# Weighted sum of two expert outputs: a store of its own for tile 0's first two tokens, and the last tile's weight load moved to another queue

## The chip, the cores and the metric

The kernel runs on one core of a Trainium2 chip. A core has several engines, each with its own instruction queue: VectorE (DVE in the profile), ScalarE (ACT), GpSimd (POOL), TensorE (PE, unused here) and SyncE (SP, which only waits and issues transfers). Transfers between the chip's main memory (HBM) and the on-chip memory with its 128 partitions are carried by 16 DMA engines, which all queues share. The metric is the device time of one execution in microseconds.

## The reference

There are 16 x 1024 = 16384 tokens. For each one the input holds two rows of 512 float32 numbers, from two experts, and two weights. The output is the weighted sum of the two rows:

```python
def reference(expert_outputs, combine_weights):   # (16,1024,2,512), (16,1024,2)
    weights = combine_weights[..., np.newaxis]
    return np.sum(expert_outputs * weights, axis=2).astype(np.float32)
```

The input is 67.1 MB, the output 33.6 MB, and a token needs 1024 multiplications and 512 additions.

## The kernel before, in words

Each partition handles 128 tokens. The first 120 of them (`main`) lie together in HBM for each partition, and are worked in ten tiles of 12 (`J`); the last eight (`LAST`) come from the end of the tensor and form tile 10, the last one. A tile `et` is 128 partitions x 12 tokens x 1024 numbers, 48 KB per partition. The pool `in` has four buffers, so tiles 0 to 3 are loaded without waiting, and the load of tile g (line 69) waits until the store of tile g-4 has landed.

All loads are issued by SP, in order (line 69). Tile 0's load is split in two: two tokens (called load 0a in what follows, rows of 4 KB) and the other ten (load 0b). All weights lie in one small tile `wt`; two transfers on ACT's queue fill it at the start (line 55): the weights of the first 120 tokens, and the 8 KB of the last tile. A warm-up ACTIVATE (line 60) follows.

Tiles 0 to 8: DVE multiplies the whole tile by the weights in place (line 78), then adds the two halves of each token (line 79). The result `ot` lies in the same buffer, packed at its front. ACT's queue issues the store (line 80), so that a store waits on DVE, and behind it wait all later stores.

Tile 9: ACT multiplies the first expert's rows, one token at a time (line 86), DVE the second's (line 101), and DVE adds (line 102). Tile 10: ACT multiplies the first expert's row of each token (line 86) and DVE multiplies and adds in one instruction (line 90). SP issues these two stores (line 103), behind all the loads. A framework orders the instructions within each queue and sets the semaphores.

Of the kernel before, what the change touches and what calls it, by code (L numbers as in the profile page):

```python
# [1 line left out]

# [4 lines left out]


@with_exitstack
def kernel(  # L10
    ctx: ExitStack,
    tc: tile.TileContext,
    expert_outputs: bass.AP,
    combine_weights: bass.AP,
    out: bass.AP,
):

    nc = tc.nc  # L20
    b, s, k, h = expert_outputs.shape
    assert k == 2
    n = b * s
    P = nc.NUM_PARTITIONS
    per = n // P
    assert per * P == n
    J, LAST = 12, 8
    main = per - LAST
    assert main % J == 0
    eo = expert_outputs.rearrange("b s k h -> (b s) (k h)")  # L30
    cw = combine_weights.rearrange("b s k -> (b s) k")
    o = out.rearrange("b s h -> (b s) h")

    def rows(x):

        a = x[0 : P * main, :].rearrange("(p t) f -> p t f", p=P)
        b = x[P * main : n, :].rearrange("(p t) f -> p t f", p=P)
        return lambda t, c: a[:, t : t + c, :] if t < main else b[:, t - main : t - main + c, :]

    eo, cw, o = rows(eo), rows(cw), rows(o)  # L40

    dt = mybir.dt.float32
    mult = mybir.AluOpType.mult
    add = mybir.AluOpType.add
    copy = mybir.ActivationFunctionType.Copy

    last = main // J

    wpool = ctx.enter_context(tc.tile_pool(name="w", bufs=1))
    ipool = ctx.enter_context(tc.tile_pool(name="in", bufs=4))  # L50

    wt = wpool.tile([P, per * k], dt)

    for t, c in ((0, main), (main, LAST)):
        nc.scalar.dma_start(
            out=wt[:, k * t : k * (t + c)].rearrange("p (t k) -> p t k", k=k), in_=cw(t, c)
        )

    warm = wpool.tile([P, 1], dt)
    nc.scalar.activation(out=warm, in_=nc.const_aps.tensor(1.0, (P, 1), dt), func=copy)  # L60

    for g in range(last + 1):
        et = ipool.tile([P, J, k * h], dt)

        ot = et.rearrange("p j f -> p (j f)")[:, 0 : J * h].rearrange("p (j f) -> p j f", f=h)
        t0, c = g * J, J if g < last else LAST

        for a, m in ((0, 2), (2, c - 2)) if g == 0 else ((0, c),):
            nc.sync.dma_start(  # L69
                out=et[:, a : a + m],  # L70
                in_=eo(t0 + a, m),
                max_dma_last_dim=k * h * 4 if g + a == 0 else None,
            )
        if g < last - 1:

            wb = wt[:, g * J * k : (g + 1) * J * k].unsqueeze(2).to_broadcast([P, J * k, h])
            ek = et.rearrange("p j (k h) -> p (j k) h", k=k)
            nc.vector.tensor_tensor(out=ek, in0=ek, in1=wb, op=mult)  # L78
            nc.vector.tensor_tensor(out=ot, in0=et[:, :, 0:h], in1=et[:, :, h : 2 * h], op=add)  # L79
            nc.scalar.dma_start(out=o(t0, c), in_=ot)  # L80
            continue


        for i in range(c):
            t = t0 + i
            nc.scalar.activation(  # L86
                out=et[:, i, 0:h], in_=et[:, i, 0:h], func=copy, scale=wt[:, 2 * t : 2 * t + 1]
            )
            if g == last:
                nc.vector.scalar_tensor_tensor(  # L90
                    out=ot[:, i, :],
                    in0=et[:, i, h : 2 * h],
                    scalar=wt[:, 2 * t + 1 : 2 * t + 2],
                    in1=et[:, i, 0:h],
                    op0=mult,
                    op1=add,
                )
        if g < last:
            w1 = wt.rearrange("p (t k) -> p t k", k=k)[:, t0 : t0 + c, 1:2]
            x1 = et[:, :, h : 2 * h]  # L100
            nc.vector.tensor_tensor(out=x1, in0=x1, in1=w1.to_broadcast([P, c, h]), op=mult)  # L101
            nc.vector.tensor_tensor(out=ot, in0=et[:, :, 0:h], in1=x1, op=add)  # L102
        nc.sync.dma_start(out=o(t0, c), in_=ot[:, 0:c])


# [1 line left out]
_INS = ['expert_outputs', 'combine_weights']  # L107
_OUTS = [((16, 1024, 512), 'float32')]


# [23 lines left out]
```

## Time and profile before

| | |
|---|---|
| median of 6 runs | 239.08 us (239.02 to 240.33) |
| profiled execution, its own time | 239.1 us |
| its span, first to last instruction | 237.3 us |
| DVE busy | 193.9 us (82%) |
| ACT busy | 14.0 us (6%) |
| DMA | 100.80 MB in 3728 packets, mean 425 GB/s |
| DVE waiting for loads (line 78) | 25.1 us, 18.5 of them at the start |
| SP's queue waiting for stores, before loads | 173.9 us |

Times in the profile are in microseconds from the start of the span. "q" after an engine's name means its instruction queue: ACTq and SPq issue transfers. In rows of instructions, "x9" is the number of them, and "et<-et,wt" names what is written and read. A transfer's time is counted from its issue to its landing, the moment when its semaphore is complete; it includes any time spent queued behind earlier transfers of the same queue.

### The profile page before, as it was taken

The numbers are of one execution on the slowest core, as the hardware profiler recorded it, in microseconds if no ns is written. First come the engines' busy times: TensorE is split into PE (matmuls) and PEld (weight loads), VectorE is DVE, ScalarE is ACT, GpSimd is POOL, SyncE is SP. The second block draws the span as 40 slices with busy tenths as digits, with TensorE's granted clock in tenths as the row PEclk, the third lists the DMA queues.
The fourth block names the chain that finished last, engine by engine and source line by source line (L and its number), as shares of the span: only waits on it lengthen the run. The fifth ranks groups of instructions, "written<-read, shape, count | busy, mean of one in ns | idle before, by whom it ended". The sixth has DMA issues, their size and how long they took to land.

```text
span 237.3 us, 154 instructions
## 1 busy us (share of the span) xinstructions
DVE 193.9 (82%) x28; ACT 14.0 (6%) x22; POOL 0.2 (0%) x4
## 2 busy tenths in 40 slices
DVE  0008999999999999999999889969996998785710
ACT  2000000000000000000000000000000000740800
POOL 0000000000000000000000000000000000000000
DMA  8999999989899999999898999999997979999997
GB/s 308 443 456 406 398 423 505 398 365 497 356 439 439 423 464 464 398 398 530 348 514 348 447 427 435 464 464 398 398 530 331 530 344 452 464 398 442 410 429 309
DMA packets 3728, 100.80 MB, mean 425 GB/s; under 512 B 528, under 2 KB 656, under 8 KB 912
## 3 DMA queue, kind: packets, MB, share of 16 engines
q1 hardware_dynamic: 2144, 72.35, 71.0%
q10 hardware_dynamic: 1584, 28.44, 27.9%
HBM read 67.24 MB, written 33.55 MB: 425 GB/s over the span
## 4 chain that ended last, share of the span: by engine, by line
DMA 59%; DVE 33%; ACT 2%; DVEq 0%; ACTq 0%; issue 0%; SPq 0%
DMA et<-in_expert_outputs_dram 30%; DMA out_dram<-et 29%; DVE et L78 22%; DVE et L79 11%; ACT et L86 2%; DVE et L90 1%; DVEq L129 0%; ACTq L129 0%; SPq L69 0%; DVEq L78 0%; ACTq L86 0%
## 5 line engine op out<-in xcount | busy, mean ns | idle before, releaser
L78 DVE TENSOR_TENSOR et<-et,wt 128x12288 f32<-128x12288 f32 x9 | 116.6, 12955 | 25.1 <-DMA et<-in_expert_outputs_dram 25.1
L79 DVE TENSOR_TENSOR et<-et 128x6144 f32<-128x6144 f32 x9 | 59.0, 6558 | 0.3
L86 ACT ACTIVATE et<-et,wt 128x512 f32<-128x512 f32 x20 | 12.5, 707 | 209.2 <-DMA et<-in_expert_outputs_dram 209.2
L90 DVE SCALAR_TENSOR_TENSOR et<-et,wt 128x512 f32<-128x512 f32 x8 | 5.6, 746 | 3.9 <-ACT et L86 3.7
L101 DVE TENSOR_TENSOR et<-et,wt 128x6144 f32<-128x6144 f32 x1 | 6.6, 6558 | 2.3 <-DMA et<-in_expert_outputs_dram 2.3
L102 DVE TENSOR_TENSOR et<-et 128x6144 f32<-128x6144 f32 x1 | 6.6, 6558 | 0.9 <-ACT et L86 0.9
L60 ACT ACT_TABLE_LOAD x1 | 1.3, 1283 | 1.7 <-PEq L118 1.7
L60 ACT ACTIVATE warm<-const-float32-1.0 128x1 f32<-128x1 f32 x1 | 0.2, 203 | 0.0
L118 POOL MEMSET const-uint8-127<- 128x1 uint8 x1 | 0.1, 103 | 0.0
L118 POOL MEMSET const-bfloat16-1.0<- 128x1 bf16 x1 | 0.1, 102 | 0.0
L118 POOL MEMSET const-float32-0.0<- 128x1 f32 x1 | 0.1, 99 | 0.2 <-issue 0.2
L118 POOL MEMSET const-float32-1.0<- 128x1 f32 x1 | 0.1, 99 | 0.0
## 6 DMA issues: line engine op xcount, KB each, us to landing
et<-in_expert_outputs_dram SPq DMA_DIRECT2D x9, 6144.0 KB, 29.9
out_dram<-et ACTq DMA_DIRECT2D x9, 3072.0 KB, 32.8
et<-in_expert_outputs_dram SPq DMA_DIRECT2D x1, 5120.0 KB, 17.2
et<-in_expert_outputs_dram SPq DMA_DIRECT2D x1, 4096.0 KB, 25.1
out_dram<-et SPq DMA_DIRECT2D x1, 3072.0 KB, 14.7
out_dram<-et SPq DMA_DIRECT2D x1, 2048.0 KB, 10.1
et<-in_expert_outputs_dram SPq DMA_DIRECT2D x1, 1024.0 KB, 5.4
wt<-in_combine_weights_dram ACTq DMA_DIRECT2D x1, 120.0 KB, 4.5
```

The costliest lines, as they stand in the source:

```text
L60: nc.scalar.activation(out=warm, in_=nc.const_aps.tensor(1.0, (P, 1), dt), func=copy)
L78: nc.vector.tensor_tensor(out=ek, in0=ek, in1=wb, op=mult)
L79: nc.vector.tensor_tensor(out=ot, in0=et[:, :, 0:h], in1=et[:, :, h : 2 * h], op=add)
L86: nc.scalar.activation(out=et[:, i, 0:h], in_=et[:, i, 0:h], func=copy, scale=wt[:, 2 * t : 2 * t + 1])
L90: nc.vector.scalar_tensor_tensor(out=ot[:, i, :], in0=et[:, i, h : 2 * h], scalar=wt[:, 2 * t + 1 : 2 * t + 2], in1=et[:, i, 0:h], op0=mul ...
L101: nc.vector.tensor_tensor(out=x1, in0=x1, in1=w1.to_broadcast([P, c, h]), op=mult)
L102: nc.vector.tensor_tensor(out=ot, in0=et[:, :, 0:h], in1=x1, op=add)
L118: nc = _bacc.Bacc("TRN2", target_bir_lowering=False, num_devices=1)
```

## The change

There are two edits, and a relabelling that goes with them.

1. In tile 0 the first two tokens are worked on their own as soon as load 0a is there: for each, ACT multiplies the first expert's row and DVE multiplies and adds the second's. Their result, 4 KB per partition, is stored by a transfer of its own on ACT's queue, cut into rows of 2 KB. The multiply, the add and the store that follow cover the ten other tokens.
2. The transfer of the last tile's weights leaves ACT's queue, where it was second, and stands on SP's queue behind the load of tile 3.

The result `ot` is now described as a view of the buffer in slots of 512 numbers, so that a part of the slots can be named. For the other tiles it is the same memory as before.

```diff
-    for t, c in ((0, main), (main, LAST)):
-        nc.scalar.dma_start(
+    def weights(q, t, c):
+        q.dma_start(
             out=wt[:, k * t : k * (t + c)].rearrange("p (t k) -> p t k", k=k), in_=cw(t, c)
         )
+
+    weights(nc.scalar, 0, main)
...
-        ot = et.rearrange("p j f -> p (j f)")[:, 0 : J * h].rearrange("p (j f) -> p j f", f=h)
+        ot = et.rearrange("p j (k h) -> p (j k) h", k=k)
...
+        if g == 3:
+            weights(nc.sync, main, LAST)
         if g < last - 1:
+            a = 0
+            if g == 0:
+                a = 2
+                for i in range(a):
+                    nc.scalar.activation(
+                        out=et[:, i, 0:h], in_=et[:, i, 0:h], func=copy, scale=wt[:, 2 * i : 2 * i + 1]
+                    )
+                    nc.vector.scalar_tensor_tensor(
+                        out=ot[:, i, :],
+                        in0=et[:, i, h : 2 * h],
+                        scalar=wt[:, 2 * i + 1 : 2 * i + 2],
+                        in1=et[:, i, 0:h],
+                        op0=mult,
+                        op1=add,
+                    )
+                nc.scalar.dma_start(out=o(t0, a), in_=ot[:, 0:a], max_dma_last_dim=h * 4)
 
-            wb = wt[:, g * J * k : (g + 1) * J * k].unsqueeze(2).to_broadcast([P, J * k, h])
-            ek = et.rearrange("p j (k h) -> p (j k) h", k=k)
+            wb = wt[:, (t0 + a) * k : (t0 + c) * k].unsqueeze(2).to_broadcast([P, (c - a) * k, h])
+            ea = et[:, a:c]
+            ek = ea.rearrange("p j (k h) -> p (j k) h", k=k)
+            oa = ot[:, 2 * a : a + c]
             nc.vector.tensor_tensor(out=ek, in0=ek, in1=wb, op=mult)
-            nc.vector.tensor_tensor(out=ot, in0=et[:, :, 0:h], in1=et[:, :, h : 2 * h], op=add)
-            nc.scalar.dma_start(out=o(t0, c), in_=ot)
+            nc.vector.tensor_tensor(out=oa, in0=ea[:, :, 0:h], in1=ea[:, :, h : 2 * h], op=add)
+            nc.scalar.dma_start(out=o(t0 + a, c - a), in_=oa)
             continue
...
-            nc.vector.tensor_tensor(out=ot, in0=et[:, :, 0:h], in1=x1, op=add)
+            nc.vector.tensor_tensor(out=ot[:, 0:c], in0=et[:, :, 0:h], in1=x1, op=add)
```

## The prediction

> **What bounds the kernel now.** I read the page first, for which engine is full.
>
> ```profile
> DVE 193.9 (82%) x28; ACT 14.0 (6%) x22; POOL 0.2 (0%) x4
> ...
> DMA  8999999989899999999898999999997979999997
> ...
> DMA packets 3728, 100.80 MB, mean 425 GB/s; under 512 B 528, under 2 KB 656, under 8 KB 912
> ```
>
> DVE is busy for 82%, the 16 DMA engines for nearly every slice. The view by stretches of time, whose last two columns are the busy share of the DMA engines and what they moved, says whether the dips to 7 are real:
>
> ```profile
> 2.00:236.00 234.00, 193.91 (x28) 13.67 (x22) 0.00 (x0) 1.00 1.00 431
> 18.00:38.00 20.00, 19.45 (x3) 0.00 (x0) 0.00 (x0) 1.00 1.00 433
> 38.00:48.00 10.00, 10.00 (x2) 0.00 (x0) 0.00 (x0) 1.00 0.97 393
> 48.00:107.00 59.00, 58.90 (x7) 0.00 (x0) 0.00 (x0) 1.00 1.00 432
> ```
>
> They are not: from 2 to 236 us the share is 1.00. Loads alone (18 to 38 us) run at 433 GB/s, loads beside stores (48 to 107) at 432. The dip at 38 to 48 us is the start of the first store. The trace also keeps each DMA packet with its start and duration. Laid end to end they leave no gap in any engine between 1.80 us (first packet) and 236.1 us (last one). So the time is the bytes over the DMA rate, with 1.8 us ahead of it and 1.2 us behind it; DVE's work counts only where it leaves the DMA with nothing to do.
>
> The timeline of DVE's large multiplies shows the rhythm: its waits for a load come every 21.7 us, and one load (6.29 MB) with one store (3.15 MB) at 434 GB/s is 21.75 us, while DVE needs 19.5.
>
> ```profile
> 115.84 12.96 DVE L78 TENSOR_TENSOR et<-et,wt 128x12288 f32<-128x12288 f32 x1
> 137.62 12.96 DVE L78 TENSOR_TENSOR et<-et,wt 128x12288 f32<-128x12288 f32 x1 [2.22 <-DMA et<-in_expert_outputs_dram]
> 159.38 12.96 DVE L78 TENSOR_TENSOR et<-et,wt 128x12288 f32<-128x12288 f32 x1 [2.21 <-DMA et<-in_expert_outputs_dram]
> 181.08 12.96 DVE L78 TENSOR_TENSOR et<-et,wt 128x12288 f32<-128x12288 f32 x1 [2.15 <-DMA et<-in_expert_outputs_dram]
> ```
>
> Last the chain that ended last (start, length, what), for how far the stores lag behind DVE and how the end is covered:
>
> ```profile
> 157.20 37.45 DMA out_dram<-et
> 194.65 0.02 SPq L69
> 194.67 0.03 issue
> 194.70 25.09 DMA et<-in_expert_outputs_dram
> ```
>
> The store issued at 157.20 takes 37.45 us. By the landings in the trace the store ahead of it in its queue landed at 172.85, so it waited 15.6 us behind that one, and then took its own 21.8. Stores thus lag DVE by 15.6 us: the cushion that covers the end. There load 10 lands at 219.79, the last store is issued 6.64 us later (226.43), and the store ahead of it lands at 231.67, 5.24 us after that issue. No engine idles.
>
> **How two queues share.** One row below settles what small rows do:
>
> ```profile
> wt<-in_combine_weights_dram ACTq DMA_DIRECT2D x1, 120.0 KB, 4.5
> wt<-in_combine_weights_dram ACTq DMA_DIRECT2D x1, 8.0 KB, 17.4
> ```
>
> 8 KB of weights, eight rows of 64 B on each engine, take 17.4 us, about as long as the 5 MB load beside them (17.2): in the packet records one row of one queue alternates with one row of the other, whatever their sizes. The completion marker of a transfer takes a turn too. Packet durations: 11 ns (64 B), 159 (4 KB), 611 (16 KB), 912 (24 KB), 1815 (48 KB), that is 9 ns and 0.0367 ns per byte.
>
> **The change, part by part.**
>
> *Bytes.* The new store has 16 rows of 2 KB on each engine. At 75 + 9 = 84 ns that is 1.35 us. Store 0 loses 4 KB from each of its eight rows, 8 x 0.150 = 1.20 us. Net +0.14 us per engine, and a marker of 0.01. Nothing hides it: the DMA is the bound.
>
> *Early ACT and DVE work.* Two ACTIVATEs (0.707 us each) and two fused multiply-adds (0.746) run after load 0a lands (0.72 + 5.4 = 6.1 us) and end near 8.5 us. Both engines were idle there (DVE until 18.51), so they cost nothing. ACT's queue then waits on DVE before the early store, with nothing behind it but store 0. If that cover were gone it would be 2.2 us of delay to store 0, which queues behind the early store anyway.
>
> *Tile 0.* Multiply and add shrink by a sixth, 19.5 to 16.3 us. Load 0b lands later by some five small rows (0.4 us, about 18.8), so DVE ends tile 0 near 35.1 instead of 38.06. The early store alternates with load rows of 1.5 to 1.8 us: 16 turns, some 29 us, done near 40. Store 0 starts there, about where it starts now (issue 38.09, first packet 43.1 by the records), ending some 2 us earlier; load 4, which now waits for both, is issued as much earlier, still 10 us before load 3 ends. No loss.
>
> *Weights of the last tile.* On ACT at 1.19 us they cost the loads nothing. Behind load 3 on SP's queue they take nine turns (eight rows and the marker) while store rows of 0.912 us take the others: the loads stand still for up to 8.2 us, the stores gain as much. The SP instruction waits for load 0a's semaphore (landed at 6.2) with load 4 behind it, which is not due before 60 us: nothing. Load 4 lands near 98 instead of 93.96, so DVE, which would end tile 3 near 94, waits some 4 us. The stores then run out, loads go alone, and that returns most of the turns. No DMA time is lost, since one queue always has rows; what is lost is most of the 15.6 us cushion.
>
> *The end.* I bound it by stores as far ahead as DVE lets them be. Let load 9 land at T. DVE ended tile 7 at T - 23.95 (T - 43.5 and 19.5), so store 7's rows run from about T - 22.5 to T - 0.7. Store 8 is issued at T + 0.3 and pairs with load 10's rows, of which one has gone. At load 10's end 0.9 to 1.8 us of store 8 is left and all of store 9 (7.3 us): 8.2 to 9.1 us of cover. Needed: 0.4 to landing, 6.64 to the issue of the last store, and 1.1 (load 0a: issue 0.72, first packet 1.80) to 2 us to its first packet: 8.1 to 9.0. So at worst a hole of about 0.8 us, at best 1 us to spare; with a few us of the lag kept, no hole. I take 0.
>
> *Unknown.* The first store made the first three load rows beside it longer, 0.56 us per engine in all, and none later. The early store now comes first: that stall may stay (0), vanish under small rows (-0.56), or come twice (+0.56). I take 0, since it came once in 11 stores, at the first.
>
> Sum on the profiled execution's own 239.1 us (span 237.3 and 1.8 around it; the median of the runs is 239.08): +0.15, hence 239.2.
>
> The Trainium skill's page "DMA: Bandwidth & Descriptors", section "Rules for kernel authors", speaks against the change: at least 1 MiB per DMA, where the new store has 0.5 MiB; its fit of a fixed 2.0 us per DMA would make 241.2. The 8 KB transfer above left no gap, so I do not charge it. The same page's section "Queues, rings and completion order" says that an engine drains a packet of some 9 to 17 descriptors from one queue before it switches; by that the early store would be over in two turns and the weights in one, the cushion would stay, and the sum would still be 239.2. The one-row turns of the records decide.
>
> **Rivals.**
> - *Small store rows stall the loads (slower).* If the stall of the first store (0.56 us in three rows, 0.19 each) comes with each of the 16 rows, +3.0 us: 242.1; with 0.05 us a row, 240.0. It decides from 0.04 us a row. For: these rows are writes set between long reads, as the first ones were. Against: every store row after the third cost nothing.
> - *A hole at the end (slower).* Nine turns lost and a worn cushion: 0 to 1.0 us, 239.2 to 240.2. For: the bound above nearly closes. Against: the stores' dry spells give turns back to the loads.
> - *The first store's stall disappears, or 2 KB rows pass beside a load row (faster).* -0.56 + 0.15 = -0.4, 238.7; all 16 rows free is another 1.2 us, 238.0 at most with one of the two. For: small rows ask little. Against: rows of 64 B and 960 B took their own time, end to end.
> - *The early store is not early* (it waits for load 0b as well): then it costs 0.15 all the same, 239.2, and only the lag changes.
>
> **How the numbers follow.** Forecast 0.50 (own range 238.9 to 239.7), stalls 0.22, hole 0.12, faster 0.13, not early 0.03. About 0.3% (0.7 us) is what a measurement of this kernel can tell from no change. Faster by more than that: half of its case, 0.07. Slower: the stalls and half of the holes, 0.28. Same: the rest, 0.65. The range leaves out the worse half of the stalls (0.11) and the better part of the faster case (0.06): 238.6 to 241.0.
>
> **What would show it.** Packets 3728 + 256 + 16 = 4000. The early store issued near 8.5 us and some 30 us on its way; the 8 KB of weights issued near 6 and landing after 75. A first multiply of 10.8 us; a DVE wait of some 4 us for load 4; stores landing sooner after their issue than the 32.8 us of now. DMA share 1.00 from 2 us to the end: if it is and the rate is 431 GB/s, the forecast holds. It is wrong if the records show load rows beside the 2 KB rows longer than 1815 ns, or a gap in the last 10 us.

## The result, and the profile after

The changed kernel takes 240.42 us (median of 24 executions, 239.53 to 242.18) against 239.05 us for the kernel before (median of 50, 238.94 to 240.82): ratio 1.0062, 95% interval 1.0049 to 1.0075. It is slower by 0.6%, and its executions scatter over 2.6 us. The kernel before has a scatter of its own: 43 of its 50 executions lie at 238.94 to 239.25 us, the other seven at 239.93 to 240.82. No execution of the changed kernel comes below 239.53. The profiled one took 240.28 us with a span of 238.5 us, 1.2 us more than before on both counts.

The page of the changed kernel, busy time by engine, the DMA engines in 40 slices, and the packets:

```profile
DVE 192.5 (81%) x30; ACT 15.3 (6%) x24; POOL 0.2 (0%) x4
...
DMA  8999999898999999999999999999999999999996
...
DMA packets 4000, 100.80 MB, mean 423 GB/s; under 512 B 544, under 2 KB 672, under 8 KB 1184
```

The bytes are the same, the packets are the 4000 that were forecast, DVE does 1.4 us less. The view by stretches, with the DMA share and GB/s in the last two columns:

```profile
2.00:236.00 234.00, 192.46 (x30) 14.47 (x24) 0.00 (x0) 1.00 1.00 430
18.00:38.00 20.00, 19.69 (x3) 0.00 (x0) 0.00 (x0) 1.00 0.95 411
38.00:48.00 10.00, 9.97 (x2) 0.00 (x0) 0.00 (x0) 1.00 0.98 413
48.00:107.00 59.00, 53.15 (x6) 0.00 (x0) 0.00 (x0) 1.00 1.02 434
```

The share from 2 to 236 us is again 1.00, the rate 430 GB/s and not 431. A full DMA thus became slower without an idle slice: that is the thing to explain. (Short stretches swing by a few per cent, since a packet is counted where it starts.)

The transfers that the change moved, each with its size and its time from issue to landing:

```profile
out_dram<-et ACTq DMA_DIRECT2D x8, 3072.0 KB, 25.5
...
out_dram<-et ACTq DMA_DIRECT2D x1, 512.0 KB, 30.8
...
wt<-in_combine_weights_dram SPq DMA_DIRECT2D x1, 8.0 KB, 71.3
```

The early store is 30.8 us on its way, the weights 71.3, and the other stores land after 25.5 us in place of 32.8: they wait less behind each other. DVE's multiplies and their waits:

```profile
98.88 12.96 DVE L100 TENSOR_TENSOR et<-et,wt 128x12288 f32<-128x12288 f32 x1 [5.02 <-DMA out_dram<-et]
...
120.71 12.96 DVE L100 TENSOR_TENSOR et<-et,wt 128x12288 f32<-128x12288 f32 x1 [2.28 <-DMA et<-in_expert_outputs_dram]
...
142.46 12.96 DVE L100 TENSOR_TENSOR et<-et,wt 128x12288 f32<-128x12288 f32 x1 [2.19 <-DMA et<-in_expert_outputs_dram]
```

DVE waits 5.0 us for load 4, which landed at 98.86 (93.96 before), 0.02 us ahead of the multiply. (The row names a store as what ended the wait, but that store landed at 99.03, after the multiply had started.) From there on DVE runs in the 21.7 us rhythm, two tiles earlier than before. The chain that ended last:

```profile
162.04 25.59 DMA out_dram<-et
187.63 0.02 SPq L71
187.65 0.03 issue
187.68 35.00 DMA et<-in_expert_outputs_dram
```

The store issued at 162.04 lands after 25.59 us, where its counterpart of before took 37.45: the store ahead of it landed at 165.80, so it waited 3.8 us and not 15.6. Load 10 lands at 222.69 (219.79 before), the last store is issued at 229.33 (226.43), 3.5 us before the landing of the store ahead of it (5.2 before).

The packet records say where the time went. Strung end to end for each of the 16 DMA engines (engines are told apart by this alone, so their numbers mean nothing from one trace to the next), they give a stall per engine, the time by which packets last longer than their usual duration, and the end of each engine. (Where packets of two engines end at the same moment the two can be exchanged; the means and the ends do not depend on that, but the stall of the worst engine can, by up to some 0.3 us.) The program's time is the end of the last engine plus 2.9 to 3.2 us in all 14 traces of this study.

| | before | changed |
|---|---|---|
| first packet | 1.80 us | 1.78 us |
| stall, 10 to 95 us, mean of the engines | 0.60 | 1.01 |
| stall after 95 us, mean / worst engine | 0.01 / 0.10 | 0.19 / 0.87 |
| end of the engines, mean | 235.92 | 236.49 |
| end of the last engine | 236.11 | 237.26 |

The mean engine ends 0.57 us later, and the last engine lies 0.77 us behind the mean where it was 0.19. Both halves make the 1.15 us. (The mean's terms, 0.41 and 0.18 of stall and 0.08 of rows, add to 0.67; the 0.1 us between is what this way of stringing packets leaves open.) No engine is idle before its last packet. Three of the 16 end at 237.0 to 237.3, one at 236.6, the others by 236.4.

### The profile page after: what moved, and what is told of

Read it like the earlier page. It is cut to its first block, busy times and chain, and to the rows that moved or that the text cites. A ratio compares the mean times of both kernels' runs of the same rounds, so it can differ in the third digit from the quotient of the medians.

```text
span 238.5 us, 161 instructions
## 1 busy us (share of the span) xinstructions
DVE 192.5 (81%) x30; ACT 15.3 (6%) x24; POOL 0.2 (0%) x4
## 4 chain that ended last, share of the span: by engine, by line
DMA 61%; DVE 32%; ACT 2%; DVEq 0%; ACTq 0%; issue 0%; SPq 0%
DMA et<-in_expert_outputs_dram 40%; DMA out_dram<-et 21%; DVE et L100 21%; DVE et L101 11%; ACT et L108 2%; DVE et L112 1%; DVEq L151 0%; ACTq L151 0%; SPq L71 0%; DVEq L100 0%; ACTq L108 0%
## 5 line engine op out<-in xcount | busy, mean ns | idle before, releaser
L100 DVE TENSOR_TENSOR et<-et,wt 128x12288 f32<-128x12288 f32 (+1 forms) x9 | 114.5, 12720 | 24.8 <-DMA et<-in_expert_outputs_dram 19.8
L101 DVE TENSOR_TENSOR et<-et 128x6144 f32<-128x6144 f32 (+1 forms) x9 | 58.0, 6439 | 0.3
L108 ACT ACTIVATE et<-et,wt 128x512 f32<-128x512 f32 x20 | 12.5, 710 | 208.0 <-DMA out_dram<-et 201.3
L124 DVE TENSOR_TENSOR et<-et 128x6144 f32<-128x6144 f32 x1 | 6.6, 6559 | 0.9 <-ACT et L108 0.9
L86 DVE SCALAR_TENSOR_TENSOR et<-et,wt 128x512 f32<-128x512 f32 x2 | 1.5, 750 | 6.8 <-ACT et L83 6.7
L112 DVE SCALAR_TENSOR_TENSOR et<-et,wt 128x512 f32<-128x512 f32 x8 | 5.6, 749 | 1.1 <-ACT et L108 0.9
L83 ACT ACTIVATE et<-et,wt 128x512 f32<-128x512 f32 x2 | 1.3, 714 | 3.2 <-DMA et<-in_expert_outputs_dram 3.2
## 6 DMA issues: line engine op xcount, KB each, us to landing
out_dram<-et ACTq DMA_DIRECT2D x8, 3072.0 KB, 25.5
```

The lines of the kernel that those rows point to most:

```text
L83: nc.scalar.activation(out=et[:, i, 0:h], in_=et[:, i, 0:h], func=copy, scale=wt[:, 2 * i : 2 * i + 1])
L86: nc.vector.scalar_tensor_tensor(out=ot[:, i, :], in0=et[:, i, h : 2 * h], scalar=wt[:, 2 * i + 1 : 2 * i + 2], in1=et[:, i, 0:h], op0=mul ...
L101: nc.vector.tensor_tensor(out=oa, in0=ea[:, :, 0:h], in1=ea[:, :, h : 2 * h], op=add)
L108: nc.scalar.activation(out=et[:, i, 0:h], in_=et[:, i, 0:h], func=copy, scale=wt[:, 2 * t : 2 * t + 1])
L112: nc.vector.scalar_tensor_tensor(out=ot[:, i, :], in0=et[:, i, h : 2 * h], scalar=wt[:, 2 * t + 1 : 2 * t + 2], in1=et[:, i, 0:h], op0=mul ...
L124: nc.vector.tensor_tensor(out=ot[:, 0:c], in0=et[:, :, 0:h], in1=x1, op=add)
```

## The experiments

All times are medians, of 12 executions each, with the lowest and the highest. They come from three sets of four kernels, each set on another chip: the four of the first part below; the four of the second; and the two of "The end" with the two of "What keeps it cheap". The kernel before had 239.05 to 239.11 us in each set of runs. The ratios are those to the kernel before in the same set. They come out closer to ratios of means than of medians, and so they are lowered by executions of the kernel before that are about 1 us late: 13 of 35 in the first set, four of 35 in the second, seven of 35 in the third. Unless a diff says otherwise, an experiment keeps the rest of the kernel before.

### The parts alone

**The early store alone**, the weights second on ACT's queue as before:

```diff
+    weights(nc.scalar, main, LAST)
...
-        if g == 3:
-            weights(nc.sync, main, LAST)
```

(against the changed kernel)

> The early store in 2 KB rows alone; the last tile's weights stay second on ACT's queue. Theory 'turns' (the weights behind load 3 take nine turns, the stores lose their lag behind DVE, and single engines then stall late): no late stall, 239.1 plus 0.14 for the small rows plus up to 0.4 for a longer stall at the first large store, 239.2 to 239.6, spread below 0.3 us. Theory 'small rows' (the early store itself disturbs the engines for the rest of the run): the whole loss, 240.0 to 240.6, with a spread of some 2 us as in the changed kernel.

Measured: 240.05 us (239.80 to 240.30), ratio 1.0022 (1.0007 to 1.0037). The stall between 10 and 95 us is 1.04 us per engine, and nothing stalls after 60 us. The time is above the forecast of 'turns' (up to 239.6) and at the low end of that of 'small rows', but the narrow spread and the absence of late stalls speak against a disturbance that lasts for the rest of the run. Neither theory has it right. The 2 KB rows take 84 ns each, all 256 of them, and the stores land 33.6 us after their issue, so the lag is whole.

**The weights behind load 3 alone**:

```diff
-    for t, c in ((0, main), (main, LAST)): ...   # both on ACT's queue
+    weights(nc.scalar, 0, main)
...
+        if g == 3:
+            weights(nc.sync, main, LAST)
```

(against the kernel before, shortened)

> The last tile's weights behind load 3 on SP's queue alone; tile 0 as before. Theory 'turns': most of the loss, 239.8 to 240.5, stores landing some 25 us after their issue in place of 32.8, late stalls of single engines in the packet records. Theory 'small rows': 239.0 to 239.2, no late stall.

Measured: 240.57 us (239.21 to 241.07), ratio 1.0044 (1.0027 to 1.0062). In the trace one engine stalls 2.1 us between 10 and 95 us where the mean is 0.72, and ends at 237.67, 1.0 us after all the others (236.48 to 236.64). That engine also delays every landing: load 10 reaches its first engine's landing at 220.34 and its last one's at 224.08, so the last store is issued at 230.72, and the other engines stand idle for 0.5 us before its rows. The "turns" theory nearly had the size (up to 240.5); but its "late stalls" were hardly there (0.2 us on the worst engine), and the single slow engine was in no theory.

**DVE's early work alone**: tile 0's first two tokens are worked early, and all twelve are stored at once.

```diff
-                nc.scalar.dma_start(out=o(t0, a), in_=ot[:, 0:a], max_dma_last_dim=h * 4)
...
-            oa = ot[:, 2 * a : a + c]
+            oa = ot[:, a:c]
...
-            nc.scalar.dma_start(out=o(t0 + a, c - a), in_=oa)
+            nc.scalar.dma_start(out=o(t0, c), in_=ot[:, 0:c])
```

(against the changed kernel, with the weights on ACT's queue)

> Tile 0's first two tokens are worked early, but stored with the other ten in one transfer of 24 KB rows; weights on ACT's queue. No small rows, DVE about 3 us earlier. Both theories: 239.0 to 239.2, since the DMA has the same rows as before. A loss here would mean that an earlier DVE alone wears the lag out.

Measured: 239.05 us (238.93 to 239.30), ratio 0.9979 (0.9961 to 0.9998), the stall 0.58 us, the last engine's end 236.18. The median is that of the kernel before. The ratio is below 1 because none of these 12 executions is late, while 13 of the 35 of the kernel before in this set lie at 239.55 to 240.97; whether the early work prevents that or 12 executions are too few to show it is open. The compute and its order cost nothing. Only the transfers do.

**The early store in rows of 4 KB**, weights on ACT's queue:

```diff
-                nc.scalar.dma_start(out=o(t0, a), in_=ot[:, 0:a], max_dma_last_dim=h * 4)
+                nc.scalar.dma_start(out=o(t0, a), in_=ot[:, 0:a])
```

(against the early store alone)

> The early store alone, in rows of 4 KB (8 on an engine and not 16), weights on ACT's queue. If the loss is by the number of small rows, it halves against the 2 KB rows; if it comes from the store being early at all, it stays. Theory 'turns': 239.1 to 239.5. Theory 'small rows': 239.5 to 240.0.

Measured: 239.89 us (239.47 to 240.18), ratio 1.0018 (1.0003 to 1.0034), stall 0.97 us per engine. This lies in the forecast of 'small rows' too, and again above that of 'turns'. But with half as many rows the loss is nearly the same, 0.78 us over the median of the kernel before and not 0.94: it does not go by the number of small rows. The stall does not lie at the small rows either. It comes at 37 to 52 us, when the first large store starts; the small one had landed at 34.0.

### Where the two costs sit

**The changed kernel again**, for a second trace:

> The changed kernel itself, for a second trace and its times beside the others. Theory 'stall and cushion' (two separate costs: some 0.4 us more stall at the first large store because a small store went ahead, and engines that fall out of step with no lag left to hide it): 240.3 to 240.6, first-store stall again 0.9 to 1.1 us per engine, while the late stalls of single engines fall elsewhere than at 172 to 224 us. Theory 'fixed places' (the late stalls belong to the addresses that meet there): the same engines 5, 6 and 14 at the same times.

Measured: 240.12 us (239.52 to 241.83), ratio 1.0035 (1.0016 to 1.0054). The stall at the first large store comes at the same places (38.4 to 38.9 and 49.1 to 49.5 us, on all 16 engines at once) with the same size, 0.92 us. The time is a little under the forecast of 'stall and cushion' (240.3 to 240.6). The late stalls of single engines come back, but at 150 to 182 us (172 to 203 in the first trace), and in both traces store rows of two or three engines stretch at 224 us, from 912 ns to between 1478 and 1942. So in these two traces the first cost is fixed and the second one wanders; that this is what scatters the times is likely but not shown, since both traced executions lie near the median. "Fixed places" holds at most for the one at 224 us.

**The changed kernel with the weights behind load 0**:

```diff
-        if g == 3:
+        if g == 0:
             weights(nc.sync, main, LAST)
```

> The changed kernel with the last tile's weights behind load 0 on SP's queue and not behind load 3, so that their nine turns fall where only loads and the early store run. Theory 'stall and cushion': the cushion's part goes and the stall stays, as with the early store alone: 239.8 to 240.2. If the weights' move costs the same from wherever SP issues it, 240.3 to 240.6.

Measured: 239.31 us (239.04 to 239.43), ratio 1.0000 (0.9986 to 1.0015). Both forecasts were too high. The stall is 0.60 us, as in the kernel before, but it lies at 14 to 18 us, at the early store's first rows; the first large store then starts without one. The engines end within 0.32 us of each other. So a store that goes early need not add to the stall, and the scatter of the changed kernel is gone. What becomes of the turns shows in two rows:

```profile
out_dram<-et ACTq DMA_DIRECT2D x1, 512.0 KB, 16.8
...
wt<-in_combine_weights_dram SPq DMA_DIRECT2D x1, 8.0 KB, 17.8
```

By the packet records the weights' rows all lie between 18.1 and 19.1 us, where the early store's 2 KB rows of 84 ns take the other turns: the two small transfers use up each other's turns. The loads stand still for 0.9 us, and the early store lands after 16.8 us and not after 30.8.

**The weights behind load 0 alone**, tile 0 as before (the diff above in the kernel with the weights alone):

> The kernel before with the last tile's weights behind load 0 on SP's queue, and nothing else. Theory 'cushion' (it is the turns beside stores that cost): 239.0 to 239.2, stores landing 32 to 33 us after their issue as before. If SP's queue or the order of issues is what costs: 240 and more, as behind load 3 (240.57).

Measured: 240.06 us (239.04 to 240.60), ratio 1.0030 (1.0013 to 1.0047), in two groups: three executions at 239.04 to 239.21, nine at 239.88 to 240.60. Two such groups are also what the kernel before shows, but there only four of 35 executions of this set are in the later one (240.05 to 240.64). The stores land 32.7 us after their issue, so the lag is whole, and the weights' rows pass at 17.3 to 17.6 us with no store beside them, so they cost no turns. Yet there is a loss: "cushion" cannot be all of it. In the trace (239.88 us) two engines stall 1.6 us where the mean is 0.82, and end at 236.93 and 236.95; the other 14 end by 236.16. No engine is idle. What costs in this trace is the longer stall, and most of all unevenness. Whether the late executions of the kernel before are of this kind is not known; none of them was traced.

**Tile 0's store cut in two, both pieces after the add**:

```diff
-            nc.scalar.dma_start(out=o(t0, c), in_=ot)
+            cut = (0, 2, c) if g == 0 else (0, c)
+            for x, y in zip(cut, cut[1:]):
+                nc.scalar.dma_start(
+                    out=o(t0 + x, y - x), in_=ot[:, x:y], max_dma_last_dim=h * 4 if y == 2 else None
+                )
```

> The kernel before with tile 0's store cut in two, 2 tokens in 2 KB rows and 10 tokens in 20 KB rows, both after the add; weights on ACT's queue. If the longer stall comes from the small transfer or from 20 KB rows ahead of the others: 1.0 us of stall per engine, 239.6 to 240.1. If it comes from the small store being early, 30 us before the large one: 0.5 to 0.6 us of stall, 239.1 to 239.3.

Measured: 239.65 us (239.42 to 239.81), ratio 1.0017 (1.0004 to 1.0029), stall 1.11 us per engine. So being 30 us early is not needed for the longer stall: a small transfer issued just ahead of a large one of 20 KB rows is enough. Which of the two does it, the small transfer or the 20 KB rows, no run separates: every kernel here with an early or a cut store has both. Here too most of the small rows pass without a stall, and it comes from 60 us on, when the last of them and the first large rows are due.

### The end

**The weights behind load 9**, just ahead of the last load:

```diff
+        if g == 9:
+            weights(nc.sync, main, LAST)
```

(the weights leave ACT's queue as before)

> The kernel before with the last tile's weights on SP's queue behind load 9, just ahead of load 10; nothing else. Theory 'cushion' (the nine turns are lost to the loads and only time spent without stores gives them back): here nothing gives them back, so load 10 lands some 4 us later and the DMA engines stand idle for 0.5 to 1.5 us ahead of the last store, 239.8 to 241. Theory 'uneven engines' (the loss behind load 3 is that of single engines that stall at the first store): no gap, 239.0 to 239.3, since the transfer comes long after that stage.

Measured: 240.70 us (239.82 to 241.42), ratio 1.0049 (1.0026 to 1.0071). Load 10 lands at 225.32, 5.5 us later than before. The tail of this kernel by stretches (DMA share and GB/s last):

```profile
224.00:230.00 6.00, 3.61 (x6) 4.58 (x8) 0.00 (x0) 1.00 0.92 397
230.00:234.00 4.00, 1.95 (x3) 0.43 (x1) 0.00 (x0) 1.00 0.57 242
234.00:236.00 2.00, 0.00 (x0) 0.00 (x0) 0.00 (x0) 1.00 1.17 492
```

and of the changed kernel:

```profile
224.00:230.00 6.00, 5.09 (x8) 3.78 (x7) 0.00 (x0) 1.00 1.07 455
230.00:234.00 4.00, 0.00 (x0) 0.00 (x0) 0.00 (x0) 1.00 0.98 420
234.00:236.00 2.00, 0.00 (x0) 0.00 (x0) 0.00 (x0) 1.00 0.95 410
```

From 230 to 234 us the share falls to 0.57, while DVE and ACT are still at the last tile: a hole of 1.6 us per engine by the packet records, with the engines ending together afterwards (237.76 to 237.90). This is the hole at the end that the "cushion" theory describes. The weights' rows took about four turns beside store rows, 3.7 us and not nine turns. The changed kernel has no hole: 0.98 there, and no gap in any engine.

**The weights behind load 3 alone, again**:

> The weights behind load 3 alone, a second time, for another trace. Theory 'cushion': 240.5 again in nearly all executions, with idle DMA time of about 0.5 us ahead of the last store's rows. Theory 'uneven engines': one engine or two with over 0.6 us more stall than the mean, perhaps other ones than engine 13, that end 0.8 to 1.2 us after the rest, whether or not there is a gap; 239.1 in the executions where no engine is late.

Measured: 240.52 us (239.24 to 242.41), ratio 1.0030 (1.0008 to 1.0053); four of the twelve at 239.24 to 239.55, one at 239.74, the rest at 240.40 and above, so not "nearly all" at 240.5. The traced execution is the slowest, 242.41 us, and no picture of the median. One engine again ends 1.0 us after the rest, and there are two gaps ahead of the last stores' rows, 1.0 us at 222 to 226 us and 1.1 at 232 to 234. Landings spread over as much as 6.5 us between the first engine's and the last one's (load 10: 219.43 and 225.90). So in this trace the two causes work together: single engines that fell behind (the worst stalls 2.25 us up to 95 us where the mean is 0.92, and the worst 1.6 after that) make the loads land late, and where the stores have little lag left, all engines wait for them.

### What keeps it cheap

**Rows of 4 KB and the weights behind load 0**:

```diff
-        if g == 3:
+        if g == 0:
...
-                nc.scalar.dma_start(out=o(t0, a), in_=ot[:, 0:a], max_dma_last_dim=h * 4)
+                nc.scalar.dma_start(out=o(t0, a), in_=ot[:, 0:a])
```

(against the changed kernel)

> The changed kernel with rows of 4 KB in the early store and the weights behind load 0. If the weights behind load 0 are what keeps the early store cheap (239.31 with 2 KB rows, against 240.05 with the weights second on ACT's queue): 239.1 to 239.3. If it was the 2 KB rows: about 239.9, as with 4 KB rows and the weights on ACT's queue.

Measured: 239.39 us (239.06 to 240.00), ratio 1.0001 (0.9984 to 1.0018). The time is near the first forecast, a little above it, and far from the second. The weights' place keeps the early store cheap, with either row length: 239.31 and 239.39 with the weights behind load 0, 240.05 and 239.89 with them on ACT's queue. (The two pairs were taken on different chips; no set of runs has both places.) The stall is 0.87 us, in two parts, at 14 to 18 us and when the first large store starts.

**The changed kernel without the last tile's weights**:

```diff
-        if g == 3:
-            weights(nc.sync, main, LAST)
...
-            t = t0 + i
+            t = t0 + i if g < last else i
```

> The changed kernel without the transfer of the last tile's weights; the last tile uses the weights of tile 0's first tokens instead, so its part of the output is another one. Theory 'two parts' (0.14 us of row overhead and 0.4 us more stall from the early store; the rest from the weights behind load 3): 239.5 to 239.8, stall near 1.0 us per engine, no stall of single engines after 60 us. If the weights have no part in it: 240.2 to 240.5 with late stalls as in the changed kernel.

Measured: 239.51 us (239.31 to 239.86), ratio 1.0007 (0.9990 to 1.0024). The stall at the first large store is 0.95 us, nothing stalls after 95 us (mean 0.01), the last engine ends at 236.61. This is the "two parts" forecast: in this kernel 0.5 us of the loss is the early store's, and the rest of it, 0.6 to 0.9 us with the scatter and the late stalls, comes in with the weights behind load 3. But the parts do not simply add. Alone, and over the median of their set, the early store with the weights on ACT's queue lost 0.94 us and the weights behind load 3 lost 1.46, together 2.4, where the changed kernel loses 1.0 to 1.4. The early store costs 0.5 us without the weights and 0.9 with them on ACT's queue; why is not known.

### All traces side by side

Stalls in us per engine; "idle" is the time that the engines stood without a packet before their last one.

| kernel | median | stall 10 to 95, mean / worst | after 95, mean | idle | last engine's end, its execution |
|---|---|---|---|---|---|
| before | 239.05 | 0.60 / 0.85 | 0.01 | 0 | 236.11, 239.1 |
| changed | 240.42 | 1.01 / 1.16 | 0.19 | 0 | 237.26, 240.28 |
| changed, again | 240.12 | 0.92 / 1.08 | 0.29 | 0 | 237.18, 240.16 |
| changed, no last weights | 239.51 | 0.95 / 1.73 | 0.01 | 0 | 236.61, 239.53 |
| changed, weights behind load 0 | 239.31 | 0.60 / 0.77 | 0.01 | 0 | 236.05, 239.04 |
| early store alone | 240.05 | 1.04 / 1.90 | 0.01 | 0 | 236.80, 240.00 |
| weights behind load 3 alone | 240.57 | 0.72 / 2.08 | 0.07 | 0.5 | 237.67, 240.59 |
| weights behind load 0 alone | 240.06 | 0.82 / 1.62 | 0.01 | 0 | 236.95, 239.88 |
| weights behind load 9 alone | 240.70 | 0.82 / 1.68 | 0.06 | 1.6 | 237.90, 240.83 |
| store cut late | 239.65 | 1.11 / 1.37 | 0.00 | 0 | 236.80, 239.78 |
| early work, one store | 239.05 | 0.58 / 0.75 | 0.01 | 0 | 236.18, 239.10 |
| early store alone, 4 KB rows | 239.89 | 0.97 / 1.44 | 0.01 | 0 | 236.82, 240.03 |
| weights behind load 3 alone, again | 240.52 | 0.92 / 2.25 | 0.26 | 2.1 | 239.49, 242.41 |
| early store in 4 KB rows, weights behind load 0 | 239.39 | 0.87 / 1.11 | 0.01 | 0 | 236.61, 239.58 |

No version has a lower median than the kernel before. The early work with one store equals it.

## Why the prediction was right or wrong

**The bound: right.** The traces are full of DMA packets (three of the 14 have 0.5 to 2.1 us of idle time, and not the changed kernel's two), and the time is the end of the last engine's packets plus 2.9 to 3.2 us. DVE's 1.4 us less brought nothing.

**The bytes: right, and smaller than forecast.** The 2 KB rows take 84 ns each and store 0's rows 761 in place of 912. The forecast was 0.14 us; neighbouring packets overlap by some 4 ns, which makes it 0.08.

**The order of events: right; the nine turns: too many.** Early store issued at 8.3 us (forecast 8.5) and landing at 39.1 (near 40); load 4 landing at 98.9 (98); DVE waiting 5.0 us for it (some 4); the weights landing at 77.2 (after 75). One row a turn is confirmed for the early store: its 16 rows went nearly one with each load row. The Trainium skill's "DMA: Bandwidth & Descriptors", section "Queues, rings and completion order", would have had the early store over after two turns; it took 30.8 us. The fixed 2.0 us per DMA that the prediction took from the same page stand there, in section "Anatomy of one DMA", for transfers issued from GpSimd. They do not show either: with one transfer more than before, all issued from ACT and SP, the kernel with the weights behind load 0 took 239.31 us against 239.08.

The weights did not take nine turns. All their rows lie between 74.5 and 76.7 us, where eight turns with store rows of 0.912 us would have taken 7.3: about three alternated with a store row, then the store beside them was over and the others passed end to end. So "up to 8.2 us" was 2.2. That load 4 still landed where it was forecast is luck: load 3 had landed 2.1 us later than before (74.28 against 72.20), as it does with the early store and no weights at all, and the weights made 2.8 us of the 4.9 (98.86 against 96.04 without them). The stores' lag fell from 15.6 to 3.8 us, as "most of the cushion" said.

**The unknown term: wrong, inside its bounds.** The step "that stall may stay (0), vanish under small rows (-0.56), or come twice (+0.56). I take 0" is the one that failed first. The stall went from 0.60 to 1.01 us per engine, +0.41. The reason given for 0, that it came once in 11 stores, at the first, does not hold when the first store is a small one: in four kernels with a small transfer ahead (the early store with the weights on ACT's queue, in 2 KB and 4 KB rows; the changed kernel without the last weights; the late cut) the stall came when the large rows behind it started, 0.95 to 1.11 us. In all four these are rows of 20 KB, so the rows may have a part in it; but with 2 KB rows in the early store and the weights behind load 0, the same 20 KB rows start with less than 0.1 us of stall.

**What was not in the sum at all.** The prediction treated the 16 engines as one. The profiled execution's last engine lies 0.77 us behind the mean (0.19 before), 0.6 us of the 1.15. In the kernel without the last weights it is 0.39, with the early store alone 0.40, so the larger part of it comes with the weights behind load 3. I had put that move at nothing but a worn cushion, and the cushion at a possible hole.

**The rivals.** "A hole at the end" did not happen in the changed kernel, but its slack was thin. The last store was issued at 229.33 us; in the three traces with a gap the first packet comes 0.84 us after that issue, so it could have started at 230.2, and the engines were free for it from 231.4 on: 1.2 us to spare, where the bound had 0.8 us too few to 1 us to spare. It did happen where the weights moved alone (0.5 us, 1.0 and 1.1 behind load 3, where an engine that is late delays the last load, and 1.6 behind load 9, where the weights' own turns do). "Small store rows stall the loads" fell: in the changed kernel the small rows pass with 1815 ns rows beside them (only six rows of 40 KB, at 12.8 to 16.0 us, are longer than usual, 0.04 us per engine in all), and half as many rows cost nearly as much. "Faster" fell as well. One run shows that its mechanism nearly works: with the weights behind load 0 the stall moves to the early store, but it does not vanish.

**The forecast.** The likeliest case, 239.2 and within 0.3%, was not what came. The range held the time, but not for the reason that it was opened upward for: it reached to 241.0 for stalls at the small rows and for a hole, and neither came. That 240.4 lies in it is luck in good part. The two signs that were to show it wrong, longer load rows beside the 2 KB rows and a gap in the last 10 us, stayed away, while the loss sat where no sign had been set. And the view that was to confirm it, a share of 1.00 at 431 GB/s, read 1.00 and 430: too coarse for a loss of 0.5%.

## What to carry to other kernels

When a profile shows a DMA that is full from start to end, as here, the time is that of the slowest of the DMA engines, so ask what makes the engines uneven and not only how many bytes they move; a mean share of 1.00 hides a microsecond on one engine. Between two queues that alternate row by row, as they do here, a transfer of few bytes costs a turn for each of its rows, but only while the other queue has rows, and as much as those rows are long: the same 8 KB held up the loads for 2.2 us in the changed kernel, beside store rows of 24 KB, for 0.9 us behind load 0 beside the rows of 2 KB, and for next to nothing where no store was under way. A late engine can cost everyone once the stores have little lag left behind the compute. A small store sent ahead of the large ones is not free because its bytes are few: where stores begin, measure the order of the transfers, since here the same parts gave 239.31 or 240.12 us, in one set of runs, by the place of one 8 KB load. And compare all executions and not the medians alone: the kernel before had between four and 13 late ones in 35.

## What was not expected of the hardware

The start of the stores holds up the loads, once: 0.6 us per engine in the kernel before, up to 1.1 in others, often on all 16 engines in the same half microsecond (all of them at 49.1 to 49.5 us in both traces of the changed kernel, when no transfer had been issued for 14 us). In no kernel did it come back on all engines after 87 us. It does not follow the count of small rows, nor the time between the small store and the large one. What it is stays open: no run here shows why it grows with a small store ahead, why it moves to the small store when the weights stand between load 0 and load 1, or why moving the weights off ACT's queue, even to a harmless place, makes most executions late (nine of 12 behind load 0, against four of 35 in the same set before), in the trace with two engines 0.8 us behind. The late stalls of single engines, at places that change between executions, are not explained either. They were seen in both traces of the changed kernel (0.9 and 1.0 us on the worst engine) and in one of the two with the weights behind load 3 alone (1.6 us). In the nine traces with the last weights elsewhere than behind load 3 or load 9, or left out, the mean after 95 us is 0.01 at most: the late stalls go with the weights behind load 3, by one trace of each kernel.
